# Softmax steps spread over three loop steps, and a gate load issued once, in a hybrid attention layer

## The chip, the cores and the metric

The kernel runs on one core of a Trainium2 chip. The metric is the device time of one execution in microseconds (us), lower is better. A core has five engines with their own instruction queues: TensorE (PE, matrix multiplications, with weight loads shown apart as PEld), VectorE (DVE), ScalarE (ACT), GpSimd (POOL) and SyncE (SP). In this kernel SP issues nearly all the DMA transfers. Each queue runs in order: an instruction that waits holds up everything behind it on its engine.

## The reference

One layer of a streaming encoder over 1024 prompt tokens and 64 new tokens of a running stream, all in float32. After a root-mean-square norm, one projection of 1024 to 6144 columns gives the queries, keys, values and a SiLU gate z for two attention branches of 8 heads of 64, and two gates per channel:

```python
h = rms_norm(x, norm_w) @ w_in
sb_q, sb_k, sb_v, sb_z, cb_q, cb_k, cb_v, cb_z, g_sb, g_cb = jnp.split(h, SPLIT_POINTS, axis=-1)
```

The first branch ("sb") is stick-breaking attention: each weight is a sigmoid times the product of (1 - sigmoid) over the keys between. The second ("cb") is softmax attention over a band of nine chunks of 64 keys with a clipped relative-position bias:

```python
s = jnp.where(mask, s + bias, NEG_INF)
p = jax.nn.softmax(s, axis=-1).astype(v.dtype)
return jnp.einsum("...hqk,...khd->...qhd", p, v)
```

The branches are merged and projected out:

```python
b_sb = (o_sb.reshape(lead + (WIDTH_SB,)) * jax.nn.silu(z_sb)) @ w_proj_sb
b_cb = (o_cb.reshape(lead + (WIDTH_CB,)) * jax.nn.silu(z_cb)) @ w_proj_cb
h = jax.nn.sigmoid(g_sb) * b_sb + jax.nn.sigmoid(g_cb) * b_cb
return x + h @ w_out
```

## The kernel before

Large matrices are split into a rounded high part and a remainder ("hi" and "lo"; `whi`, `wlo`, `xa`, `xm`, `xb`), and each product is three matrix multiplications: hi by hi, hi by lo, lo by hi. ScalarE makes the hi part of a weight tile (L115), GpSimd or VectorE subtracts to get the lo part (L122).

The kernel runs in this order: input projections (to about 398 us), then one long loop over attention tiles, then the second branch's projection (L926), then the output projection (L1429, L1465). What concerns us is the loop. Its list `seq` holds first all tiles of the first branch and then 68 tiles of the second: four pairs of heads, for each the 64 new tokens (t = 8) and eight blocks of 128 queries for each of two heads. In the code each loop step i does, in this order:

- `qk(i)`: the scores of tile i into PSUM (L1035). For the second branch VectorE takes them out of PSUM, adds bias and finds the running minimum (L1041, in two halves when the tile has over 512 keys; bias and queries carry a minus sign, so that the minimum stands for the softmax's maximum), and ScalarE makes the exponential in place with its sum (L1045). The tile is called `be`, the small statistics tile `sm`.
- `mid(i - 1)`: for the first branch the scan and the product (L1055, L1056), for the second the reciprocal of the sum (L1058) and the scaling of the tile (L1059).
- `fill`: a number of matrix multiplications of other work, taken one after another from a generator, so that TensorE has something to do while a tile is on its way through the other engines. The generator first runs the rest of the input projection (L782, results `sg`), and then `proj_sb`, the projection of the first branch's output (L882).
- `av`: when a block of queries is complete, weights times values (L1126) and the product with z (L1131), stored to DRAM (`d_ocb`).
- `tr(i - 3)`: TensorE transposes tile i - 3 (L1087), ScalarE and VectorE take turns copying it out of PSUM (L1096, L1098).
- the rest of the step's `fill`.

The `be` tiles have four buffers, the score tiles in PSUM (`z`) three, the transposed tiles (`pt`) two.

`proj_sb` goes through twelve pieces j, four pairs of column blocks by three stretches of tokens (384, 384 and 320). Each piece has two halves `uu`, each of twelve matrix multiplications into one of two PSUM accumulators (`acc`), which VectorE multiplies by the gate (L886) into a large tile `xm`. The gate tile `gt` of a piece, two blocks wide, comes back from DRAM (`d_gsb`, L862, by `load_gate`) in two DMAs. The tile has two buffers. `proj_sb` calls `load(j + 1)` twice: at the start of piece j, and again after the first half. Each call allots a tile and issues its two DMAs; the second call's tile is the one that piece j + 1 reads.

When the attention loop is done, what is left of `proj_sb` is filled in between loading the second branch's output (`ot`, L839) and splitting it into hi (L843, ScalarE) and lo (L848, by turns GpSimd and VectorE), for three stretches of tokens. The tile `ot` has two buffers there. These loads stand on the same SP queue as the gates', and the VectorE subtractions L848 stand on the same queue as the multiplications L886. In the built program the order on VectorE there is: L886 of piece 9 (first half), two L848, L886 of piece 9 (second half), L886 of piece 10 (first half), two L848, L886 of piece 10 (second half), two L886 of piece 11, two L848.

Of the kernel before, what the change touches and what calls it, by code (L numbers as in the profile page):

```python
# [10 lines left out]
AF = mybir.ActivationFunctionType  # L11
# [21 lines left out]
def hybrid_step_kernel(ctx: ExitStack, tc: tile.TileContext, x_prompt, x_sample, c_sbk, c_sbv, c_cbk, c_cbv,  # L33
# [3 lines left out]
    V, A, G, TE, SP = nc.vector, nc.scalar, nc.gpsimd, nc.tensor, nc.sync  # L37
# [15 lines left out]
    def rows(t):  # L53
        return 128 if t < 8 else NS
# [46 lines left out]
    class Weights:  # L101
# [5 lines left out]
        def load(self, key, pool, src, shape, extra="", nx=1):  # L107
            raw = pool.tile(shape, F32, name="wraw" + extra, bufs=nx if extra else 2)
            SP.dma_start(raw, src)
            self.raw[key] = (raw, pool, shape, extra)  # L110
# [87 lines left out]
    with ExitStack() as ph:  # L198
# [251 lines left out]
        for i in range(nb):  # L450
            for ti, t in enumerate(TO):
                r = rows(t)
# [91 lines left out]
    with ExitStack() as ph:  # L544
# [70 lines left out]
        for i in range(len(pairs)):  # L615
            bank, s1, u2, u3 = {}, {}, {}, {}
            for s in range(7):
                n = 7 * i + s
# [92 lines left out]
    SQ, KS, VP, BI, st, wT, zts = {}, {}, {}, {}, {}, {}, {}  # L711
# [98 lines left out]
    def og(b, s, p):  # L810
        return xhl[s][s][:, p] if b == "sb" else late["og"][s][:, p]

    def tb(u):
        return late["tbt"][:, u]
# [43 lines left out]
    def load_gate(pool, name, key, us, ci):  # L858
        a, e = CH[ci]
        gts[key] = pool.tile([128, 2, 384], F32, name=name, bufs=2)  # L860
        for w, d in enumerate(us):
            SP.dma_start(gts[key][:, w, :e - a], d[:, a:e])  # L862

    def proj_sb(pool):
        load = lambda j: j < 12 and load_gate(pool, "gt", j, d_g["sb"][2 * (j // 3):2 * (j // 3) + 2], j % 3)
        for j in range(12):
            i, ci = divmod(j, 3)
            wh, wl = W.sp["p", i]
            a, e = CH[ci]
            load(j + 1)  # L870
            if ci == 0:
                load_proj(i + 2)
            if ci == 1:
                W.split(("p", i + 1))
            gt = gts.pop(j)
            for uu in range(2):
                cw = slice(uu * 128, uu * 128 + 128)
                ps = psF.tile([128, 512], F32, name="acc")
                for p in range(NPAIR):
                    gh, gl = og("sb", 0, p), og("sb", 1, p)  # L880
                    for m, (w, g) in enumerate(((wh, gh), (wh, gl), (wl, gh))):
                        TE.matmul(ps[:, :e - a], w[:, p, cw], g[:, a:e], start=p == 0 and m == 0,  # L882
                                  stop=p == NPAIR - 1 and m == 2)
                        if p < NPAIR - 1 or m < 2:
                            yield 1
                V.tensor_tensor(out=tb(2 * i + uu)[:, a:e], in0=ps[:, :e - a], in1=gt[:, uu, :e - a], op=OP.mult)  # L886
                if uu == 0:
                    load(j + 1)
                yield 1

    def load_gcb(j):
# [95 lines left out]
    def fill(n):  # L987
        n += owed[0]
        owed[0] = 0
        while n > 0:  # L990
# [9 lines left out]
    seq = [(b, p, t, hd) for b in ("sb", "cb") for p in range(NPAIR) for t in [8] + list(range(8))  # L1000
           for hd in range(2) if t < 8 or hd == 0]

    def band(b, t):
        if t == 8:
            return 0, 576
        if b == "sb":
            return 0, (t + 1) * 128
        k0 = max(0, t - 4)
        return k0, (t + 1 - k0) * 128

    def qk(i):
        b, p, t, hd = seq[i]
        key = (b, p)
        r = 128
        k0, n = band(b, t)
        hs = [(0, n)] if n <= 512 else [(0, n // 2), (n // 2, n)]
        be = am.tile([128, NP], F32, name="be", bufs=4)
        if t == 8:
            s, ks, q0 = SQ[key, 3], KS[key, 1], 0
        else:  # L1020
            s, ks, q0 = SQ[key, t // 3], KS[key, 0], (t % 3) * 128
        if b == "sb":
            kp = ax.tile([128, NP + 2], F32, name="kp", bufs=3)
            G.memset(kp[:r, n:n + 1], 0.0)
        else:
            kp = am.tile([128, 4], F32, name="sm", bufs=6)
            bt = BI[2 * p + hd] if t < 8 else BI["s", p]
            off = 0 if t == 8 else 640 - n
        for j, (x, y) in enumerate(hs):
            z = psZ.tile([128, 512], F32, name="z")  # L1030
            o = k0 * 128
            m = y - x
            parts = [(2 * h + e, h) for h in ((0, 1) if t == 8 else (hd,)) for e in range(2)]
            for e, h in parts:
                TE.matmul(z[:, :m], s[:, e, q0:q0 + 128], ks[:, h, o + x:o + y], start=e == parts[0][0],  # L1035
                          stop=e == parts[-1][0])
            if b == "sb":
                A.activation(kp[:r, x:y], z[:r, :m], AF.Sigmoid, scale=-0.125)
                A.activation(be[:r, x:y], z[:r, :m], AF.Sigmoid, scale=0.125)
            else:  # L1040
                V.tensor_tensor_reduce(be[:r, x:y], z[:r, :m], bt[:r, off + x:off + y], 1.0,  # L1041
                                       BIG if j == 0 else kp[:r, j - 1:j], OP.add, OP.min, kp[:r, j:j + 1])
        if b == "cb":
            j = len(hs) - 1
            A.activation(be[:r, :n], be[:r, :n], AF.Exp, bias=kp[:r, j:j + 1], scale=-1.0, accum_out=kp[:r, 2:3])  # L1045
        st[i] = (be, kp)

    def mid(i):
        b, p, t, hd = seq[i]
        r = 128  # L1050
        k0, n = band(b, t)
        be, kp = st[i]
        if b == "sb":
            im = ims[:] if t == 8 else imp[:, NP - n:NP]
            V.tensor_tensor_scan(kp[:r, n - 1::-1], kp[:r, n - 1::-1], im[:, ::-1], 0.0, op0=OP.mult, op1=OP.add)  # L1055
            V.tensor_tensor(out=be[:r, :n], in0=be[:r, :n], in1=kp[:r, 1:n + 1], op=OP.mult)  # L1056
        else:
            V.reciprocal(kp[:r, 3:4], kp[:r, 2:3])  # L1058
            V.tensor_scalar(be[:r, :n], be[:r, :n], kp[:r, 3:4], None, op0=OP.mult)  # L1059
# [41 lines left out]
    def load_z(b, p, j):  # L1101
        zt = am.tile([128, 256], F32, name="zt", bufs=3)
        nq = 256 if j < 4 else 64
        SP.dma_start(zt[:, :nq], d_z[b][p][:, 256 * j:256 * j + nq])
        zts[b, p, j] = zt
# [53 lines left out]
    def load_bias(h):  # L1159
        bt = ab.tile([128, 640], F32, name="bias", bufs=4)  # L1160
        src = d_rb[h][0:1, 127:128]
        SP.dma_start(bt, bass.AP(tensor=src.tensor, offset=src.offset, ap=[[767, 128], [1, 640]]))
        G.memset(bt[0:64, 576:640], BIG)
        G.memset(bt[64:128, 0:64], BIG)
        BI[h] = bt
        if h % 2:
            bs = BI["s", h // 2] = ab.tile([128, 576], F32, name="bsm", bufs=1)
            for w in range(2):
                src = d_rb[h - 1 + w][0:1, 127:128]
                SP.dma_start(bs[64 * w:64 * w + 64], bass.AP(tensor=src.tensor, offset=src.offset,  # L1170
                                                             ap=[[767, 64], [1, 576]]))
# [16 lines left out]
    for i in range(len(seq) + LAG + 1):  # L1188
        m = 0
        if i < len(seq):  # L1190
            b, p, t, hd = seq[i]
            if b == "cb" and p == 0 and t == 8 and hd == 0:
                sbx.close()
                yst = ExitStack()
                late["y"] = yst.enter_context(tc.tile_pool(name="ay", bufs=2))
            if (b, p, t, hd) == ("sb", 3, 6, 0):
                load_bias(0)
                load_bias(1)
            qk(i)
            if hd == 0:  # L1200
                if t % 2 == 1 or t == 8 and (b, p) != ("sb", 0):
                    load_z(b, p, t // 2 if t < 8 else 4)
                prefetch(b, p, t)
            acc += amount[b] * wt[b](band(b, t)[1]) / tot[b]
            if (b, p, t) == ("cb", 0, 8):
                acc += 12
            m = int(acc) - emitted
            emitted += m
        if 0 < i <= len(seq):
            mid(i - 1)  # L1210
        flush()
        if i < len(seq) and seq[i][:3] == ("cb", 0, 1) and hd == 1:
            late["sb"] = True
        fill(m // 2)
        while avq:
            av(*avq.pop(0))
        if 0 <= i - LAG < len(seq):
            tr(i - LAG)
            b, p, t, hd = seq[i - LAG]
            if t == 8 or hd == 1 and t % 2 == 1:  # L1220
                avq.append((b, p, t // 2 if t < 8 else 4))
        fill(m - m // 2)
# [117 lines left out]
    hs = ow1.tile([128, KT, 128], F32R, name="hs", bufs=1)  # L1340
# [61 lines left out]
    for i in range(2):  # L1402
# [3 lines left out]
        for q, s in enumerate(OP_):  # L1406
            n = 8 * i + q
# [48 lines left out]
            for s_, wh, wl in ([] if n == 0 else [(0,) + first, (3, wh, wl)] if n == 1 else  # L1456
                               [(s, wh, wl)] if s in (0, 3, "b", 5) else []):
                w = 0 if s_ in (0, 3) else 1
                r = 0 if s_ in (0, "b") else 1
# [55 lines left out]
```

## Time and profile before

| | us |
|---|---|
| median of 3 runs | 998.18 (997.74 to 999.14) |
| the profiled execution | 996.75 |
| its span in the profile | 995.0 |
| TensorE busy | 971.9 |
| VectorE busy | 655.2 |
| ScalarE busy | 461.0 |
| GpSimd busy | 325.5 |

The lines L... in a profile are those of the kernel before. A group's row names the line, the engine, the operation, the tile written and the tiles read. A number in square brackets behind a row of the timeline is the time that the engine stood idle before it, and whose end released it. "PEclk" and "granted clock" give the share of its full clock that TensorE was granted. "SPq" is the queue of SyncE. A row of the view of waits gives the total, the number and the longest of a kind of wait. Start times in the timeline are counted from the start of the span.

### The profile page before, as it was taken

To read this page: it belongs to the slowest core of one execution; us is meant where nothing else is said; L and a number is where in the kernel's file an instruction comes from. 1 tells how busy PE (TensorE), PEld (TensorE's weight loads), DVE (VectorE), ACT (ScalarE), POOL (GpSimd) and SP (SyncE) were. 2 spreads that over 40 slices of the span, in tenths; PEclk is the share of its full clock that TensorE was granted. 3 is DMA by queue.
4 is the path that set the end of the run, shared out by engine and by line. 5 is a ranking of instruction groups with operands and counts; after the bars stand their busy time and mean duration, and the time that the engine had idled before them with its cause. 6 is when DMAs were issued, how large, how long until landed. Compare 5 with 4: busy or idle time off the path is not lost.

```text
span 995.0 us, 20010 instructions
## 1 busy us (share of the span) xinstructions
PE 971.9 (98%) x7472; PEld 928.7 (93%) x7472; DVE 655.2 (66%) x1200; ACT 461.0 (46%) x1038; POOL 325.5 (33%) x336
## 2 busy tenths in 40 slices
PE   5999999999999999999999999999999999899998
PEld 5999999999999999989988889899989898799998
DVE  5456674795455554189787988576657774589745
ACT  5534443444344433277676656444444433365320
POOL 3276663215445543211111101120103102286641
PEclk9999999999999999999999999999999999999999
DMA  6726577434656332697565657575667754852732
GB/s 228 234 93 222 190 245 254 153 97 138 200 151 197 113 95 83 176 237 199 142 172 158 165 155 193 136 200 149 188 183 236 226 162 149 265 172 93 214 125 84
DMA packets 181506, 171.02 MB, mean 172 GB/s; under 512 B 35040, under 2 KB 167264, under 8 KB 181280
## 3 DMA queue, kind: packets, MB, share of 16 engines
q1 hardware_dynamic: 172688, 161.41, 54.2%
q10 hardware_dynamic: 8720, 8.33, 2.6%
q8 instruction: 59, 0.97, 0.4%
q14 instruction: 39, 0.32, 0.1%
HBM read 110.96 MB, written 58.72 MB: 171 GB/s over the span
## 4 chain that ended last, share of the span: by engine, by line
PE 93%; DVE 2%; DMA 2%; ACT 1%; issue 1%; POOL 0%; SPq 0%; DVEq 0%; ACTq 0%
PE acc L464 19%; PE acc L782 18%; PE b L634 17%; PE b L1429 8%; PE o L1126 7%; PE z L1035 7%; PE pt L1087 6%; PE b L926 5%; PE acc L882 4%; DVE kp L1055 1%; PE pk L349 1%; DMA wrawx<-in_w_in_dram 1%; PE pt L277 1%; PE acc L1465 1%; PE acc L595 0%
## 5 line engine op out<-in xcount | busy, mean ns | idle before, releaser
L122 POOL TENSOR_TENSOR wlo<-wraw,whi 128x1024 fp32r<-128x1024 f32 x30 | 73.5, 2451 | 235.2 <-ACT whi L115 221.5
L782 PE MATMUL acc<-xm,whi 128*128 128x384 f32 (+1 forms) x384 | 129.1, 337 | 0.0
L1087 PE MATMUL pt<-ident,be 128*128 128x128 f32 (+1 forms) x568 | 87.6, 278 | 4.1 <-DVE wT L1098 3.0
L1055 DVE TENSOR_TENSOR_SCAN kp<-kp,imp 128x128 f32<-128x128 f32 (+7 forms) x64 | 90.0, 1407 | 0.1
L1045 ACT ACTIVATE be<-be,sm 128x640 f32<-128x640 f32 (+5 forms) x68 | 47.7, 702 | 89.3 <-DVE sm L1041 54.5
L1035 PE MATMUL z<-ks,sq 128*128 128x320 f32 (+5 forms) x384 | 83.3, 325 | 0.0
L1096 ACT ACTIVATE wT<-pt 128x512 f32<-128x512 f32 (+3 forms) x125 | 57.9, 477 | 54.0 <-PE pt L1087 53.4
L1087 PEld LDWEIGHTS pt<-ident,be 128*128 128x128 f32 (+1 forms) x568 | 66.4, 140 | 14.6 <-issue 5.3
L464 PE MATMUL acc<-whi,xa 128*128 128x256 f32 x256 | 74.2, 292 | 0.0
L782 PEld LDWEIGHTS acc<-xm,whi 128*128 128x128 f32 x384 | 72.4, 189 | 1.1
L464 PE MATMUL acc<-wlox,xm 128*128 128x256 f32 x256 | 70.7, 278 | 0.0
L464 PE MATMUL acc<-whi,xm 128*128 128x256 f32 x256 | 70.7, 278 | 0.0
L464 PE MATMUL acc<-wlo,xa 128*128 128x256 f32 x256 | 70.7, 278 | 0.0
L464 PE MATMUL acc<-whix,xb 128*128 128x256 f32 x256 | 70.6, 278 | 0.0
L464 PE MATMUL acc<-whix,xm 128*128 128x256 f32 x256 | 70.6, 278 | 0.0
L1035 PEld LDWEIGHTS z<-ks,sq 128*128 128x128 f32 x384 | 65.6, 188 | 1.1
L1056 DVE TENSOR_TENSOR be<-be,kp 128x128 f32<-128x128 f32 (+8 forms) x68 | 59.2, 871 | 9.1
L1126 PE MATMUL o<-wT,vp 128*64 128x256 f32 (+1 forms) x608 | 65.1, 356 | 0.0
L782 PE MATMUL acc<-xa,whi 128*128 128x384 f32 (+1 forms) x192 | 64.7, 337 | 0.0
L782 PE MATMUL acc<-xa,wlo 128*128 128x384 f32 (+1 forms) x192 | 64.6, 337 | 0.0
L782 PE MATMUL acc<-xb,whi 128*128 128x384 f32 (+1 forms) x192 | 64.4, 335 | 0.0
L782 PE MATMUL acc<-xm,wlo 128*128 128x384 f32 (+1 forms) x192 | 64.4, 335 | 0.0
(300 smaller groups left out, 2919.5 us busy)
## 6 DMA issues: line engine op xcount, KB each, us to landing
wraw<-in_w_in_dram SPq DMA_DIRECT2D x35, 512.0 KB, 4.7
wrawx<-in_w_in_dram SPq DMA_DIRECT2D x13, 512.0 KB, 4.4
sq<-d_qsbT SPq DMA_DIRECT2D x32, 192.0 KB, 4.2
sq<-d_qcbT SPq DMA_DIRECT2D x32, 192.0 KB, 3.6
gt<-d_gsb SPq DMA_DIRECT2D x30, 192.0 KB, 3.1
xt<-in_x_prompt_dram SPq DMA_DIRECT2D x8, 512.0 KB, 5.6
d_kcbT<-hl SPq DMA_DIRECT2D x8, 512.0 KB, 4.5
d_qcbT<-hl SPq DMA_DIRECT2D x8, 512.0 KB, 5.2
```

The costliest lines, as they stand in the source:

```text
L122: (eng or G).tensor_tensor(out=l, in0=raw, in1=h[:].bitcast(F32), op=OP.subtract)
L464: TE.matmul(ps, x, w, start=m == 0, stop=m == len(steps) - 1)
L634: TE.matmul(ps[:, :m], w[:, hl_, k], right[s](x)[:, k, a:b], start=s < 3 and k == 0 and e == 0, stop=k == 3 and e == 2, skip_group_check=s ...
L782: TE.matmul(ps[:, :b - a], w[:, k], xk(x, k)[:, a:b], start=k == 0 and n == 0, stop=k == KT - 1 and n == 2)
L926: TE.matmul(pp[uu][:, :n], w[:, p, uu * 128:uu * 128 + 128], g[:, a:e], start=p == 0 and m == 0, stop=p == NPAIR - 1 and m == 2)
L1035: TE.matmul(z[:, :m], s[:, e, q0:q0 + 128], ks[:, h, o + x:o + y], start=e == parts[0][0], stop=e == parts[-1][0])
L1055: V.tensor_tensor_scan(kp[:r, n - 1::-1], kp[:r, n - 1::-1], im[:, ::-1], 0.0, op0=OP.mult, op1=OP.add)
L1056: V.tensor_tensor(out=be[:r, :n], in0=be[:r, :n], in1=kp[:r, 1:n + 1], op=OP.mult)
L1087: TE.transpose(pt[:kr, x, :r], be[:r, kb * 128:kb * 128 + kr], ident[:r, :r])
L1096: A.activation(w[:, sl:sl + m, q0:q0 + r], pt[:, :m, :r], AF.Copy)
L1126: TE.matmul(o[hd * 64:hd * 64 + 64, c0:c1], vv[:kr, kb, hd * 64:hd * 64 + 64], wT[b, p, j, hd, s // 4][:kr, s % 4, c0:c1] if j < 4 else wT ...
L1429: TE.matmul(ps[:, t], left[s](xs_, k)[:, ts_], wt_[:, k], start=s < 3 and t == k == e == 0, stop=k == 3 and e == 2, skip_group_check=s > 2 ...
```

## The change

In the second branch, the exponential leaves `qk` and becomes a function of its own, `soft`, which the loop calls for tile i - 1 before `qk(i)`. The second branch's `mid` is called for tile i - 2, also before `qk(i)`. For the first branch `mid(i - 1)` keeps its place behind `qk(i)`. The transposes stay at `tr(i - 3)`. So on ScalarE's queue the exponential of a tile stands one step later than before, ahead of the next tile's work; on VectorE's queue the reciprocal and the scaling of a tile stand one step later, and ahead of the bias and minimum of tile i, not behind them.

In `proj_sb`, the second `load(j + 1)` is taken out: 22 of the 46 DMAs that read `d_gsb`. The order of the instructions on TensorE and on GpSimd is the same as before.

```diff
                 V.tensor_tensor(out=tb(2 * i + uu)[:, a:e], in0=ps[:, :e - a], in1=gt[:, uu, :e - a], op=OP.mult)
-                if uu == 0:
-                    load(j + 1)
                 yield 1
...
-        if b == "cb":
-            j = len(hs) - 1
-            A.activation(be[:r, :n], be[:r, :n], AF.Exp, bias=kp[:r, j:j + 1], scale=-1.0, accum_out=kp[:r, 2:3])
         st[i] = (be, kp)
+
+    def soft(i):
+        n = band(*seq[i][::2])[1]
+        be, kp = st[i]
+        j = 1 if n > 512 else 0
+        A.activation(be[:, :n], be[:, :n], AF.Exp, bias=kp[:, j:j + 1], scale=-1.0, accum_out=kp[:, 2:3])
...
+        if 0 < i <= len(seq) and seq[i - 1][0] == "cb":
+            soft(i - 1)
+        if 1 < i <= len(seq) + 1 and seq[i - 2][0] == "cb":
+            mid(i - 2)
+        if i < len(seq):
             qk(i)
...
-        if 0 < i <= len(seq):
+        if 0 < i <= len(seq) and seq[i - 1][0] == "sb":
             mid(i - 1)
         flush()
```

## The prediction

> **What bounds the kernel now.** I read the page first: its shares by engine, then the chain that ended last.
>
> ```profile
> span 995.0 us, 20010 instructions
> PE 971.9 (98%) x7472; PEld 928.7 (93%) x7472; DVE 655.2 (66%) x1200; ACT 461.0 (46%) x1038; POOL 325.5 (33%) x336
> PE 93%; DVE 2%; DMA 2%; ACT 1%; issue 1%; POOL 0%; SPq 0%; DVEq 0%; ACTq 0%
> ```
>
> TensorE is busy for 971.9 of 995.0 us. A change that leaves its matmuls as they are can only win from the 23.1 us in which it stands still, or from matmuls that run at a lower clock. So I next asked for the busy time by stage (second branch's attention, last part of the first branch's projection, second projection, output projection) and for whom TensorE waits.
>
> ```profile
> 613.00:836.00 223.00, 220.44 (x1604) 200.82 (x1604) 150.55 (x440) 101.12 (x241) 32.36 (x28) 1.00 0.63 181
> 836.00:860.00 24.00, 19.45 (x115) 17.88 (x112) 8.63 (x14) 5.02 (x9) 6.42 (x5) 0.96 0.69 213
> 860.00:910.00 50.00, 50.00 (x308) 50.00 (x308) 43.01 (x57) 29.88 (x51) 33.55 (x27) 0.98 0.54 170
> 910.00:995.00 85.00, 81.06 (x716) 80.86 (x714) 50.33 (x62) 22.21 (x30) 37.33 (x16) 1.00 0.44 140
> ...
> PE acc L882 <- DVE xm L886: 4.5, 4, 3.2
> PE pt L1087 <- DVE wT L1098: 1.7, 3, 1.1
> PE pt L1087 <- ACT wT L1096: 0.9, 2, 0.5
> ```
>
> Columns of the first rows: stretch, length, then busy time of PE, PEld, DVE, ACT and POOL, granted clock, DMA share, GB/s. The change touches the first two stretches. In them TensorE idles 223.00 - 220.44 = 2.56 us and 24.00 - 19.45 = 4.55 us. The last rows say on whom: 4.5 us in four waits of the first branch's projection (L882) for the gate multiplication (L886), 1.7 + 0.9 us in the attention for copies out of PSUM. Nothing else on TensorE is to be had: 7.1 us, and what the clock loses.
>
> **Part one: each gate loaded once.** The multiplication L886 needs its gate tile, and the two accumulators of L882 come free only after it. The four waits, the DMA queue beside them, and the chain through this place:
>
> ```profile
> L862 SPq DMA_DIRECT2D gt<-d_gsb x46: 319/422/998, 752.4 to 855.9; - x46
> 845.89 0.45 PE L882 MATMUL acc<-xa,whi 128*128 128x384 f32 x1 [0.51 <-DVE xm L886]
> 848.55 0.44 PE L882 MATMUL acc<-xa,whi 128*128 128x384 f32 x1 [0.30 <-DVE xm L886]
> 851.50 0.41 PE L882 MATMUL acc<-xa,whi 128*128 128x320 f32 x1 [0.57 <-DVE xm L886]
> 856.68 0.41 PE L882 MATMUL acc<-xa,whi 128*128 128x320 f32 x1 [3.16 <-DVE xm L886]
> 840.53 0.43 SPq L862 DMA_DIRECT2D gt<-d_gsb  x1
> 841.74 3.45 DMA gt<-d_gsb
> 844.28 1.36 SPq L862 DMA_DIRECT2D gt<-d_gsb  x2
> 848.52 0.81 SPq L862 DMA_DIRECT2D gt<-d_gsb  x2
> 849.43 1.80 SPq L839 DMA_DIRECT2D ot<-d_ocb  x4
> 849.85 3.75 DMA ot<-d_ocb
> 853.62 1.57 ACT L843 ACTIVATE og<-ot 128x384 fp32r<-128x384 f32 x3 [0.84 <-DMA ot<-d_ocb]
> 845.75 2.27 DVE L848 TENSOR_TENSOR og<-ot,og 128x384 fp32r<-128x384 f32 x2
> 844.76 2.38 POOL L122 TENSOR_TENSOR wlo<-wraw,whi 128x1024 fp32r<-128x1024 f32 x1 [0.94 <-ACT whi L115]
> ```
>
> The 46 issues are 2 for the first gate tile and 2 x 2 for each of the 11 others; 22 of them go. Read in time: the first copy of gate 9 is issued until 840.96, its second copy at 841.74, and this second copy, in flight for 3.45 us, holds the multiplication until 845.28. The first copy of gate 10 is issued at 844.28, so gate 9's first copy had landed by about then. The second copy of gate 10 is issued at 848.52, and only behind it the four tiles of the second branch's output (849.43, ot). The last of these, 3.75 us in flight by the chain, lands at 853.60. Then ScalarE rounds, VectorE subtracts (L848), and in VectorE's order the next L886 stands behind that subtraction: it starts at 856.09, 2.49 us after the landing, and TensorE has stood still for 3.16 us.
>
> With one copy: gate 9 is there by 844.28, its multiplication 1.0 us earlier, and the 0.51 wait goes. Gate 10's only copy takes the place at 841.74 and lands, at the same 3.45 us, by 845.2. The first half of gate 10's matmuls ran from 845.89 to 848.25 (848.55 less the wait of 0.30); without the 0.51 they end at about 847.7, so that copy is hidden. The ot tiles wait only for their buffers, that is for the two subtractions L848 now at 845.75 to 848.02. These start 1.0 earlier too, but the second shares its time with POOL's L122 (844.76 to 847.14), which doesn't move, so its end lies between 847.0 and 848.0. The second pair of ot, whose last issue was at 850.80 (849.43 + 1.80 less one issue of 0.43), now has it at 847.5 to 848.5; with 2.8 us (853.60 - 850.80) to 3.75 us in flight it lands at 850.3 to 852.2, between 1.4 and 3.3 us earlier. Add the same 2.49 us: TensorE resumes 1.4 to 3.3 us before 856.68. I take 2.8, nearer the upper end, since the trace's own last transfer took 2.8. TensorE's wait there shrinks to about 1.3 us, because the 0.57 wait before it goes as well and its work ends earlier. The wait of 0.30 stays. The second copies of gates 1 to 8 lie in the attention, where no wait of TensorE is put down to L886; taking them out wins nothing there.
>
> A second effect lies behind it:
>
> ```profile
> 784.00:786.00 2.00, 1.10 (x8) 1.10 (x9) 1.97 (x8) 0.45 (x3) 0.06 (x1) 1.00 0.95 267
> 858.00:859.00 1.00, 1.00 (x6) 1.00 (x6) 0.28 (x1) 0.00 (x0) 0.00 (x0) 0.61 0.98 306
> 859.00:860.00 1.00, 1.00 (x4) 1.00 (x4) 0.49 (x1) 0.00 (x0) 0.00 (x0) 0.50 0.89 266
> 860.00:861.00 1.00, 1.00 (x4) 1.00 (x4) 0.00 (x0) 0.88 (x1) 0.00 (x0) 0.50 0.87 283
> 861.00:862.00 1.00, 1.00 (x5) 1.00 (x5) 0.00 (x0) 0.99 (x2) 0.00 (x0) 0.68 0.91 280
> ```
>
> About 1.4 us after the long wait the granted clock falls to half for some 3.4 us: 0.39 + 0.50 + 0.50 + 0.32 = 1.71 us of TensorE's work lost. A wait of 1.06 us (784 to 785) left it at 1.00. The wait I forecast, 1.3 us, is far nearer 1.06 than 3.16, so I take the 1.7 us as won, with 0 as the other end. [...]
>
> Downstream the lead must survive. From 860 to 910 TensorE never waits (50.00 of 50.00), but VectorE is nearly full there (43.01). The tightest place:
>
> ```profile
> 922.21 2.40 POOL L1292 TENSOR_TENSOR wo<-wo,wo 128x1024 fp32r<-128x1024 f32 x1 [4.37 <-ACT wo L1291]
> 920.34 16.32 PE b L1429 x144
> ```
>
> POOL's weights are done at 924.61. In this run of 144 matmuls (16.32 / 144 = 0.113 us each) TensorE needs them in the 51st, at 926.0: 1.4 us of slack. The chain of gates and ot behind POOL's work comes 2.8 earlier, TensorE 2.8 + 1.7 = 4.5; the difference of 1.7 overruns the slack by 0.3. I charge 0.2 (0 to 0.3).
>
> **Part two: the exponential one step later, the normalising two.** No instruction is added; none on SP or POOL moves, and TensorE's order is unchanged.
>
> ```profile
> ACT be L1045 <- DVE sm L1041: 54.5, 45, 2.5
> DVE be L1041 <- PE z L1035: 40.8, 50, 2.0
> L1045 ACT ACTIVATE be<-be,sm x68: 401/777/837, 616.3 to 827.6; 128x640 f32<-128x640 f32 x32, 128x128 f32<-128x128 f32 x8, 128x256 f32<-128x256 f32 x8, 128x384 f32<-128x384 f32 x8
> L1059 DVE TENSOR_SCALAR be<-be,sm x68: 285/553/2501, 621.2 to 831.2; 128x640 f32<-128x640 f32 x32, 128x128 f32<-128x128 f32 x8, 128x256 f32<-128x256 f32 x8, 128x384 f32<-128x384 f32 x8
> L115 ACT ACTIVATE whi<-wraw 128x1024 fp32r<-128x1024 f32 x10 | 10.5, 1049 | 0.0
> 782.13 2.25 DVE L1059 TENSOR_SCALAR be<-be,sm 128x576 f32<-128x576 f32 x1
> 781.69 2.38 POOL L122 TENSOR_TENSOR wlo<-wraw,whi 128x1024 fp32r<-128x1024 f32 x1 [2.68 <-ACT whi L115]
> 784.90 0.44 PE L1087 MATMUL pt<-ident,be 128*128 128x128 f32 x2 [1.06 <-DVE wT L1098]
> 623.46 1.14 PE L1087 MATMUL pt<-ident,be 128*128 128x128 f32 x8 [0.52 <-ACT wT L1096]
> ```
>
> Now ScalarE stands at each exponential until VectorE has the minimum of the same step (54.5 us), with its PSUM copies (L1096) queued behind; VectorE waits 40.8 us for the scores. Afterwards the exponential finds its minimum a step old, and the scaling runs while VectorE would wait for scores. A step lasts 223 / 68 = 3.3 us, the exponential at most 0.84, the scaling 0.55 in the median: the transposes, still three steps behind, find their tile scaled a step ahead. The move costs nothing while that slack covers it; without it, at the end of the branch where no projection fills the steps, one exponential and one scaling (1.4 us) could show once. What is won is bounded by the 2.56 us. 0.52 hangs on ScalarE's queue and should go. 1.06 hangs on a scaling stretched to 2.25 us beside POOL's subtraction: the order behind it changes (next the score evacuation, then the copy), so it can go or come back at another step (the L115 row counts 10 weight tiles rounded in this stage, each followed by such a pass of POOL). The rest are the emptied steps at the end. I take 0.5 (ends: 2.6 won, 2 lost by two more such collisions of 1.06).
>
> **Sum.** 2.8 + 1.7 + 0.5 - 0.2 = 4.8 us. The profiled execution took 996.75 us (span 995.0), so 992.0. The timed runs have their median at 998.18, 1.43 above it: 993.4.
>
> **Rivals.**
> 1. The clock falls all the same. Short waits remain close together, 0.30 and 1.3. [...] For it: the dip came 1.4 us after the resumption, so it is not tied to one wait alone. Against: many small waits in the attention at clock 1.00. Then the 1.7 isn't won and the 0.2 isn't charged: 998.18 - 3.3 = 994.9. Chance 0.14.
> 2. The gates are early but something else holds the multiplication: the ot tiles, or POOL's L122 beside L848. For it: the 3.16 wait ends on ot, not on a gate. Then only 0.51 + 0.57 go, the clock still dips, and the attention gives 0 to 0.5: about 997.0. Chance 0.13.
> 3. Slower: in the attention POOL's L122 (10 passes) meets the scaling in every pass, as in 782.13, and what stands behind it is now the evacuation of the scores and the copies. If each pass costs 1.06 us on TensorE, that is 10.6 less the 1.6 already paid: 9.0 lost against 4.3 won elsewhere, 998.18 + 4.7 = 1002.9. It decides from six such passes on (6 x 1.06 is more than 4.3 + 1.6). Against: scalings of up to 2.50 us are there now, and all of TensorE's waits for copies are 2.6 us. Chance 0.07.
> 4. All waits of both stretches go: 7.1 + 1.7 = 8.8, 989.4. Chance 0.10. That the change doesn't do what it says is excluded for the gates by the 46 issues.
>
> **How the numbers follow.** My forecast has 0.56; its own range, from the ends of its terms (2.8: 1.4 to 3.3; 0.5: -1 to 1.5; 1.7), is 991.5 to 996.3. The whole range must leave out no more than 2 in 10: up to 997.0 for rival 2, down to 990.5 for half of rival 4. A measurement of this kernel tells 0.2%, 2 us, from no change. Faster, below 996.2: forecast, rivals 1 and 4, and a little of 2: 0.81. Same: most of rival 2: 0.11. Slower: rival 3 and accidents: 0.08.
>
> **What would show it.** 24 gate issues in place of 46; TensorE's waits for L886 at 2 us or less in place of 4.5 and the longest under 2; granted clock 1.00 after the last of them; ScalarE's wait of 54.5 near nothing; TensorE's waits in the attention at 2.6 or less. The forecast is wrong if the ot tiles land no earlier, if the clock dips, or if waits for PSUM copies grow past 4 us.

## The result and the profile after

The changed kernel takes 990.14 us (median of 4 runs, 989.93 to 992.98). Beside it on the same chip the kernel before took 998.4 (997.74 to 999.14). The ratio is 0.9924 with a 95% interval of 0.9904 to 0.9943: 8.3 us faster, where 4.8 were forecast. The unaltered kernel run again later on another chip gave 991.31 (988.84 to 994.83), ratio 0.9931 (0.9913 to 0.9948). The profiled execution took 989.93, with a span of 988.1 where the one before had 995.0. That profile of the kernel before is one of its faster executions (996.75, against medians of 998.2 to 998.7), so the spans differ by less (6.9) than the medians.

The page of the kernel after: span, busy times, and the shares of the chain that ended last.

```profile
span 988.1 us, 20002 instructions
PE 968.8 (98%) x7472; PEld 927.1 (94%) x7472; DVE 649.3 (66%) x1200; ACT 458.4 (46%) x1038; POOL 325.1 (33%) x336
PE 93%; DMA 3%; DVE 2%; SPq 1%; issue 0%; POOL 0%; ACT 0%; DVEq 0%; ACTq 0%
```

TensorE carries the same work (x7472) and still bounds the kernel. The stages (columns as before the change):

```profile
613.00:836.00 223.00, 222.15 (x1622) 203.12 (x1621) 144.46 (x441) 99.24 (x241) 32.45 (x28) 1.00 0.59 168
836.00:860.00 24.00, 21.30 (x129) 21.04 (x128) 9.60 (x16) 9.06 (x16) 9.04 (x7) 1.00 0.73 220
860.00:910.00 50.00, 50.00 (x333) 50.00 (x332) 46.68 (x58) 30.01 (x53) 36.68 (x28) 1.00 0.55 172
```

TensorE's idle time is 0.85 us in the attention (2.56 before) and 2.70 in the tail (4.55). The granted clock stays at 1.00 in these stages. Who waits for whom, the first row over the span and the others in the window 613 to 836:

```profile
PE acc L882 <- DVE xm L886: 2.7, 1, 2.7
...
PE pt L1088 <- DVE wT L1099: 0.4, 1, 0.4
PE pt L1088 <- ACT wT L1097: 0.4, 1, 0.4
ACT be L1047 <- DVE sm L1039: 8.8, 10, 1.9
DVE be L1039 <- PE z L1033: 22.2, 36, 2.0
ACT wT L1097 <- PE pt L1088: 87.5, 44, 4.8
```

Four waits for the gate multiplication have become one, and the waits for copies out of PSUM have fallen from 1.7 + 0.9 us to 0.4 + 0.4. ScalarE's 54.5 us at the exponential (now L1047) are 8.8, and VectorE's 40.8 us for scores are 22.2. ScalarE's idle time hasn't gone, it has moved: it now waits 87.5 us for the transposes (25.2 before), where it holds up nobody.

To place the gain I cut the span at three landmarks on TensorE: the second branch's first scores, the start of its last weights-times-values, and the first matmul of the second projection. The timeline of the kernel before, then of the kernel after:

```profile
614.44 1.21 PE L1035 MATMUL z<-kss,sqs 128*128 128x288 f32 x8
834.48 2.81 PE L1126 MATMUL o<-wT,vp 128*64 128x256 f32 x24
858.79 0.84 PE L926 MATMUL b<-og,whi 128*128 128x384 f32 x2
```

```profile
614.25 1.21 PE L1033 MATMUL z<-kss,sqs 128*128 128x288 f32 x8
832.05 2.81 PE L1127 MATMUL o<-wT,vp 128*64 128x256 f32 x24
853.45 0.51 PE L924 MATMUL b<-og,whi 128*128 128x384 f32 x2
```

The stretch between the first two landmarks is called the attention below, the next the tail, and what follows the rest. The attention went from 220.04 (834.48 - 614.44) to 217.80, the tail from 24.31 to 21.40, the rest, to the end of the span, from 136.21 to 134.65. The gain of 6.9 in the span is 0.2 before the first landmark + 2.2 + 2.9 + 1.6. The same stretches of every kernel below, each from its one profiled execution:

| kernel | median | ratio (95%) | attention | tail | rest |
|---|---|---|---|---|---|
| before | 998.4 | | 220.04 | 24.31 | 136.21 |
| after | 990.14 | 0.9924 (0.9904, 0.9943) | 217.80 | 21.40 | 134.65 |
| after_again | 991.31 | 0.9931 (0.9913, 0.9948) | 218.86 | 20.77 | 135.50 |
| gate_only | 992.60 | 0.9946 (0.9934, 0.9958) | 220.04 | 20.63 | 135.04 |
| gate_late | 993.03 | 0.9945 (0.9929, 0.9961) | 220.48 | 20.52 | 135.66 |
| soft_only | 996.79 | 0.9984 (0.9975, 0.9992) | 217.59 | 26.90 | 135.64 |
| before_keepwarm | 996.61 | 0.9980 (0.9971, 0.9989) | 220.03 | 24.47 | 134.81 |
| exp_only | 992.23 | 0.9939 (0.9922, 0.9956) | 220.08 | 20.61 | 135.05 |
| scale_behind | 993.45 | 0.9953 (0.9938, 0.9969) | 220.77 | 20.56 | 134.67 |
| scale_first | 997.02 | 0.9986 (0.9975, 0.9996) | 224.07 | 20.30 | 134.65 |
| before_split_v | 998.98 (one run) | | 220.09 | 25.54 | 136.86 |
| og_later | 989.47 | 0.9910 (0.9897, 0.9923) | 217.71 | 18.44 | 135.53 |
| og_later_again | 988.41 | 0.9899 (0.9885, 0.9913) | 217.83 | 18.45 | 134.96 |

The ratios are against runs of the kernel before on the same chip, whose medians were 998.4 to 998.7. The two profiles of the changed kernel differ by 1.1 in the attention and 0.6 in the tail: differences below that say nothing by themselves. Over all profiles the attention is 217.6 to 218.9 in the five that have both moves of the softmax, and 220.0 to 220.5 in the five that have neither. Line numbers in the experiments are shifted by a few against the kernel before or after.

### The profile page after: what moved, and what is told of

It is laid out like the page before. It is cut to its first block, busy times and chain, and to the rows that moved or that the text cites. A ratio compares the mean times of both kernels' runs of the same rounds, so it can differ in the third digit from the quotient of the medians.

```text
span 988.1 us, 20002 instructions
## 1 busy us (share of the span) xinstructions
PE 968.8 (98%) x7472; PEld 927.1 (94%) x7472; DVE 649.3 (66%) x1200; ACT 458.4 (46%) x1038; POOL 325.1 (33%) x336
## 4 chain that ended last, share of the span: by engine, by line
PE 93%; DMA 3%; DVE 2%; SPq 1%; issue 0%; POOL 0%; ACT 0%; DVEq 0%; ACTq 0%
PE acc L464 19%; PE acc L782 18%; PE b L634 17%; PE b L1435 8%; PE o L1127 7%; PE z L1033 6%; PE pt L1088 6%; PE b L924 5%; PE acc L882 3%; DMA gt<-d_gsb 1%; DVE kp L1056 1%; PE pk L349 1%; DMA wrawx<-in_w_in_dram 1%; PE pt L277 1%; PE acc L1471 1%; DMA ot<-d_osb 1%
## 5 line engine op out<-in xcount | busy, mean ns | idle before, releaser
L1036 ACT ACTIVATE kp<-z 128x384 f32<-128x384 f32 (+6 forms) x104 | 51.2, 493 | 27.3 <-PE z L1033 26.2
```

## The experiments

**The two parts apart.** The gate part alone, and the softmax part alone:

```diff
# gate_only, against before
-                if uu == 0:
-                    load(j + 1)
# soft_only, against after
+                if uu == 0:
+                    load(j + 1)
```

> The change's first part alone: the second load of each gate is taken out, the softmax steps stay where they were. Theory (the two parts add up): all of the tail's gain is here. TensorE resumes 2.8 us earlier in the last piece of the first branch's projection, its longest wait for the gate multiplication is about 2.7 us in place of 3.16, the granted clock stays at 1.00 behind it, worth another 1.7 us; the attention keeps its waits of 0.52 and 1.06. Span 995.0 - 4.5 = 990.5, median 993.7. Rival (the tail is gained only because the shorter attention shifts the queues against each other): the long wait stays near 3.2, the clock dips, and the span is 993 or more.

> The change's second part alone: exponential one step and normalising two steps later, each gate still loaded twice. Theory: the waits of 0.52 and 1.06 in the attention go, the last product with the values starts 2.4 us earlier than before, the tail stays as before with its 3.16 us wait and the clock dip. Span 995.0 - 2.4 = 992.6, median 995.8. Rival (the gate loads' traffic and queue made the attention's gain): the waits stay, span 994 to 995.

The gates alone give 6.0 us (998.58 beside it, to 992.60), the softmax part alone 1.8. The sum, 7.8, is near the 8.3 measured for both. The gates' gain lies where it was forecast: tail 24.31 to 20.63, rest 136.21 to 135.04, attention unchanged. The wait that is left there is 1.93 us, shorter than the 2.7 I expected. In the softmax part alone the attention wins 2.45, but with the second copies still there its profiled execution gives it all back in the tail. The timeline, the waits, two transfers from the chain and two windows of soft_only there (the windows between, all near 0.50, left out):

```profile
856.09 0.63 PE L882 MATMUL acc<-xa,whi 128*128 128x320 f32 x1 [4.04 <-DVE xm L886]
```

```profile
PE acc L882 <- DVE xm L886: 6.2, 3, 4.0
```

```profile
840.18 4.97 DMA gt<-d_gsb
...
848.03 5.02 DMA ot<-d_ocb
```

```profile
854.00:855.00 1.00, 0.00 (x0) 0.00 (x0) 0.60 (x2) 0.55 (x2) 0.84 (x1) 0.56 0.04 13
...
860.00:861.00 1.00, 1.00 (x4) 1.00 (x4) 0.19 (x1) 0.99 (x2) 0.00 (x0) 0.53 0.65 218
```

TensorE came to the tail 1.9 sooner (832.56 for 834.48), but the loads hardly did: issued earlier, they were 5 us in flight and landed at 845.15 and 853.05, where before it was 845.19 and 853.60. So the waits for L886 grew from 4.5 to 6.2, and half the clock was gone from 854 to 861. The two spans are equal (995.0 and 995.1), yet the median falls by 1.8: the profile of the kernel before is a fast execution of it (996.75, median 998.58 beside this run), that of soft_only an average one (996.87, median 996.79). So how often the tail takes the gain back isn't shown.

**Which of the two copies.** The first call taken out and the second kept:

```diff
# gate_late, against before
-            load(j + 1)
```

> The kernel before with one load of each gate, but the other one: the call at the start of a piece is out, the call after the first half stays. Theory (what costs is the second copy, which holds the queue until the first has landed or the buffer comes free, with the other loads behind it): as good as taking out the second call, median 992 to 993.5, granted clock 1.00 behind the longest wait. Rival (what counts is that the load that is read comes half a piece earlier): the gates come late as before, waits for the gate multiplication of 4 us or more, median 996 to 998.

The tail takes 20.52, as in gate_only (20.63), and the ratios are equal within their intervals. It isn't the earlier place that wins; a second copy ahead of `ot` in the queue is what cost. SyncE's own waits from 765 to 862 us, in the kernel before and then after, show how:

```profile
SPq L862 <- DMA gt<-d_gsb: 18.4, 12, 2.9
```

```profile
SPq L862 <- DMA gt<-d_gsb: 0.2, 1, 0.2
```

Twelve times SyncE stood with a gate load until another gate load had landed, 18.4 us in all, with everything behind it held. It isn't the lighter traffic: in the window 835 to 860 the median time from issue to landing of the 192 KB loads has risen, from 3.3 to 4.3 us for `ot` and from 3.5 to 4.9 for the gates.

**The clock.** The kernel before with 14 unread matmuls put into the long wait; nothing reads their PSUM tile, and the multiplication that TensorE waits for stays where it is:

```diff
# before_keepwarm, against before
+NDUM = 14
...
+                if j == 11 and uu == 1:
+                    dm = late["dum"].tile([128, 512], F32, name="dum")
+                    for m in range(NDUM):
+                        TE.matmul(dm[:, :e - a], wh[:, 0, cw], og("sb", 0, 0)[:, a:e], start=m == 0, stop=m == NDUM - 1)
...
```

> The kernel before, with 14 matmuls more ahead of the last half piece of the first branch's projection, into a PSUM tile that nobody reads. They take 14 x 0.147 = 2.1 us and fit into the 3.16 us in which TensorE stands still there, so that it resumes at the same time but has idled only about 1.1 us. Theory (the half clock follows from the length of that wait): the granted clock stays at 1.00 and the second projection starts at full rate, 1.7 us won: span 993.3, median 996.5. Rival (the dip has another cause): the clock falls to half as before and the span is 995.0 or more.

A window of before_keepwarm:

```profile
858.00:860.00 2.00, 2.00 (x14) 2.00 (x15) 0.51 (x2) 0.00 (x0) 0.00 (x0) 1.00 0.89 264
```

TensorE's wait there is 1.20 us in place of 3.16. The clock stays at 1.00, the tail is as long as before (24.47), and the rest is shorter by 1.40. So the idle stretch caused the dip, and the dip cost about 1.4 in this profile (2.0 by the medians), where I had worked out 1.71. In two of its ten timed runs the mean clock is 0.998 all the same.

**What carries the attention's gain.** Two theories. A: ScalarE's queue; its PSUM copies stood behind an exponential that waited for the minimum. B: VectorE's order; it must not have a late scaling between the scores and what TensorE waits for. exp_only takes just the exponential a step later; scale_behind takes both later as the change does, but puts the scaling behind the minima; scale_first leaves the exponential in its step and puts only the scaling ahead of the next minima.

```diff
# exp_only, against after
-        if 1 < i <= len(seq) + 1 and seq[i - 2][0] == "cb":
-            mid(i - 2)
...
-        if 0 < i <= len(seq) and seq[i - 1][0] == "sb":
+        if 0 < i <= len(seq):
             mid(i - 1)
# scale_behind, against after
-        if 1 < i <= len(seq) + 1 and seq[i - 2][0] == "cb":
-            mid(i - 2)
         if i < len(seq):
             qk(i)
...
+        if 1 < i <= len(seq) + 1 and seq[i - 2][0] == "cb":
+            mid(i - 2)
# scale_first, against after
         if 0 < i <= len(seq) and seq[i - 1][0] == "cb":
-            soft(i - 1)
-        if 1 < i <= len(seq) + 1 and seq[i - 2][0] == "cb":
-            mid(i - 2)
+            mid(i - 1)
         if i < len(seq):
             qk(i)
+            if seq[i][0] == "cb":
+                soft(i)
```

> The changed kernel, but reciprocal and scaling go back to their old place: one step after the scores, behind the bias and minimum of the next tile; only the exponential is a step later. Measure: the time from the first scores of the second branch to its last product with the values, 220.0 us with the old order (before, and with the gates alone changed), 217.6 to 217.8 with the new one. Theory A (what counts is that ScalarE's copies no longer stand behind an exponential that waits for VectorE): 217.8 here too, span as the changed kernel's. Theory B (what counts is VectorE's order, the stretched scalings no longer ahead of the copies): 219 to 219.5, the wait of 1.06 near 785 us comes back, and the median is 1.2 to 1.7 above the changed kernel's.

> The changed kernel, but the reciprocal and scaling, still two steps after the scores, stand behind the bias and minimum of the newest tile on VectorE, not ahead of them. Theory A (ScalarE's queue): 217.8 from first scores to last product. Theory B (place on VectorE, since a scaling stretched beside GpSimd's subtraction then stands right ahead of the copies out of PSUM again): 218.5 to 219.5, with a wait of about 1 us near 785.

> The changed kernel with the exponential put back into its own step, behind the minimum; only the reciprocal and the scaling stay ahead of the next tile's minima on VectorE (one step later than before, not two). If the place of the scaling on VectorE alone makes the gain in the attention: the stretch from the branch's first scores to its last weights-times-values takes 217.5 to 218.3 us as in the changed kernel (217.80), and the time is within 1 us of it (989.5 to 991). If it needs both, the scaling ahead and a step between exponential and scaling: VectorE now waits at the head of each step for the exponential of the step before, and the stretch takes 219.5 to 220.5 us, the time 992 to 993.

None of the three has the attention's gain: 220.08, 220.77 and 224.07 against 217.80, each from one profile and each longer than my theories allowed (219.5, 219.5 and 220.5 at most). Theory A as I held it falls with exp_only: ScalarE was freed, the wait of 0.52 at 623 went, and the stretch is as long as before. Its medians are also no better than the gate part alone (992.23 and 992.60). In scale_behind the transposes wait for the scaling itself; its waits and timeline:

```profile
PE pt L1088 <- DVE be L1060: 1.2, 2, 0.8
```

```profile
780.22 2.74 DVE L1060 TENSOR_SCALAR be<-be,sm 128x640 f32<-128x640 f32 x1
```

But theory B alone falls too, with scale_first, which moves the scaling ahead and loses 4 us. Its waits in the window 613 to 838, and a row of its VectorE timeline:

```profile
ACT be L1047 <- DVE sm L1039: 96.0, 65, 3.0
...
DVE sm L1059 <- ACT be L1047: 12.6, 18, 1.1
```

```profile
785.50 2.48 DVE L1060 TENSOR_SCALAR be<-be,sm 128x576 f32<-128x576 f32 x1
```

Here VectorE stands at the head of a step for the exponential (12.6 us), the next minima come later for it, and ScalarE waits 96.0 us for these. TensorE's waits for the copies of the transposed tiles come to 4.8 us in this window (2.6 before), the longest, 1.6, ends at 788.71, shortly behind the scaling at 785.50, which is stretched to 2.48. What wins is the pair: the scaling ahead of the minima, and the exponential a step before it, so that nobody stands for it. I can't name every part of what exp_only loses: up to 799 us it is ahead of the kernel before by 1.0 and loses that again by the end, and in that last part the profile lists, beyond a wait of 0.36 that both kernels have, only waits of 0.20 and 0.58 (0.39 before).

**The stretched scaling.** The wait of 1.06 at 784.90 hung on a scaling beside a pass of POOL. The next kernel is the one before with that one pass moved from POOL to VectorE:

```diff
# before_split_v, against before
-                W.split(("p", i + 1))
+                W.split(("p", i + 1), V if i == 0 else None)
```

> The kernel before, with one of the weight subtractions moved from GpSimd to VectorE: the one that runs from 781.69 to 784.07 beside the scaling of 2.25 us. Theory (GpSimd's pass stretches the scaling, and that makes TensorE's wait of 1.06 at 784.90): no scaling over 1 us there, the wait gone or below 0.3 although VectorE has 1.2 us more to do, first scores to last product 219.0. Rival (the scaling was stretched by something else, or the emptied short steps alone make the wait): the wait stays near 1, 220.0 or more.

The timeline of before_split_v at that place:

```profile
781.91 1.22 DVE L122 TENSOR_TENSOR wlo<-wraw,whi 128x1024 fp32r<-128x1024 f32 x1 [0.46 <-ACT whi L115]
...
784.05 0.52 DVE L1059 TENSOR_SCALAR be<-be,sm 128x576 f32<-128x576 f32 x1
...
783.79 0.44 PE L1087 MATMUL pt<-ident,be 128*128 128x128 f32 x2 [1.15 <-DVE wT L1098]
```

The scaling takes 0.52 us in place of 2.25, so POOL's pass did stretch it. But the wait stays (1.15), because the subtraction now takes 1.22 us of VectorE right ahead of the copy that TensorE waits for (783.05 to 783.73). The run shows the cause of the stretch; whether the wait would go with neither in the way it can't tell. In the kernel after the stretch is still there, without a wait at its place (timeline, VectorE then POOL):

```profile
779.50 2.17 DVE L1060 TENSOR_SCALAR be<-be,sm 128x640 f32<-128x640 f32 x1
...
778.93 2.39 POOL L122 TENSOR_TENSOR wlo<-wraw,whi 128x1024 fp32r<-128x1024 f32 x1 [1.65 <-ACT whi L115]
```

In after_again a wait for a copy came back there, 0.91 us long, and that profile's attention is 1.1 longer.

**The wait that is left.** In the kernel after, the rest of `proj_sb` taken out wholly ahead of the second pair of `ot` splits, so that L886 no longer stands behind L848; and the same once more beside the unaltered change:

```diff
# og_later, against after
-        fill((46, 24, 100000)[ci])
+        fill((46, 100000, 0)[ci])
```

> The changed kernel, with the rest of the first branch's projection put ahead of the splitting of the second stretch of the second branch's output, so that VectorE's gate multiplications no longer stand behind the subtractions that wait for that load. Theory: the wait of 2.70 us that the changed kernel still has goes, or shrinks to what the last gate's load takes: span 988.1 - 2 to 2.7 = 985.4 to 986, median about 988. Rival: the second projection then waits for the split that comes later, at its second piece, and the span stays at 988.

> The changed kernel unaltered, for a comparison on one chip. Both theories: 989.5 to 991.5 us.

> The changed kernel with the rest of the first branch's projection taken out wholly ahead of the second pair of output tiles' splits, as in og_later. If the 0.7 us between the medians of og_later and the changed kernel is more than scatter: 988.5 to 990, 0.5 to 1.2 below the changed kernel beside it. If the wait taken away comes back in full behind it: the same to 0.3 us.

The stage rows of og_later_again:

```profile
836.00:860.00 24.00, 24.00 (x147) 24.00 (x147) 9.63 (x19) 9.80 (x17) 8.62 (x7) 1.00 0.71 218
860.00:910.00 50.00, 50.00 (x339) 50.00 (x338) 45.81 (x59) 30.20 (x54) 37.89 (x28) 1.00 0.55 172
```

TensorE doesn't wait in the tail at all. Side by side the medians are 988.41 and 991.31; in the first comparison, which was not side by side, 989.47 and 990.14. The intervals of the two pairs still meet (0.9913 on the last chip), so the gain of some 1 to 3 us is likely, not certain. One thing speaks for it besides: the mean granted clock is 1.000 in all eight timed runs of it, and 0.998 in four of the ten of the changed kernel. It is the fastest version here.

## Why the prediction was right, and where its sizes were off

The direction, the cause and the place were right; the size was not. I forecast 993.4 and measured 990.14, just below my low end of 990.5 (the repeat, 991.31, lies inside). Of the 3.3 us missing, 1.7 are the attention's term. Another 1.2 come from the step from profile to median: I added 1.43, as before, but the profiled execution after lies only 0.2 below its median. What that step is made of no run here shows. The other terms make up the remaining 0.4.

**Gate term, 2.8.** Measured 2.9 in the tail of the pair of profiles, 3.7 in gate_only. The mechanism held: the gates are issued once, and `ot` no longer stands behind a second copy. The issues (grouped by line), then the tail's timeline, of the kernel after:

```profile
L862 SPq DMA_DIRECT2D gt<-d_gsb x24: 319/423/1731, 751.9 to 845.6; - x24
```

```profile
851.59 0.41 PE L882 MATMUL acc<-xa,whi 128*128 128x320 f32 x1 [2.70 <-DVE xm L886]
848.84 2.23 DVE L848 TENSOR_TENSOR og<-ot,og 128x384 fp32r<-128x384 f32 x2 [3.19 <-ACT og L843]
850.99 0.94 DVE L886 TENSOR_TENSOR xm<-acc,gt 128x384 f32<-128x384 f32 x2
847.77 2.04 ACT L843 ACTIVATE og<-ot 128x384 fp32r<-128x384 f32 x4 [5.13 <-DMA ot<-d_ocb]
842.83 2.08 SPq L839 DMA_DIRECT2D ot<-d_ocb  x4
845.06 0.82 SPq L862 DMA_DIRECT2D gt<-d_gsb  x2
```

TensorE resumes 5.09 us earlier (851.59 for 856.68), 2.43 of it because the attention ended earlier; that leaves 2.66, close to 2.8. The steps inside were off, and cancelled. The issue of `ot` in gate_only, whose attention is as long as before:

```profile
845.57 1.76 SPq L839 DMA_DIRECT2D ot<-d_ocb  x4
```

I had the last `ot` issue at 847.5 to 848.5; it was at 846.90 (845.57 + 1.76 less one issue of 0.43). But I took 2.8 us in flight, which I had read wrongly: the landing at 853.60 belongs to the load issued at 849.85, 3.75 us earlier, not to the last issue at 850.80. In the kernel after the first of them lands 4.9 us after its issue (847.77 - 842.83). Behind it ScalarE's four roundings now stand back to back (2.04): only the first has a wait ahead of it. The multiplication still stands behind L848, as forecast.

**"The wait shrinks to about 1.3 us, and the 0.30 stays."** Wrong. The 0.30 went with the 0.51 and the 0.57, TensorE came to the last half piece 2.20 earlier in the tail instead of 1.1, and so it stood 2.70 there (3.16 - 2.66 + 2.20). Of these 2.20, 1.38 are the three waits as listed. The other 0.8 is what a break costs beyond its listed wait. TensorE's timeline before, around the first of the three:

```profile
845.04 0.34 PE L882 MATMUL acc<-xa,wlo 128*128 128x384 f32 x1
845.89 0.45 PE L882 MATMUL acc<-xa,whi 128*128 128x384 f32 x1 [0.51 <-DVE xm L886]
846.17 0.34 PE L882 MATMUL acc<-xb,whi 128*128 128x384 f32 x1
```

In an unbroken stream matmuls of 384 columns start some 0.17 us apart, each before the one ahead has ended. Here two starts are 0.85 apart and the next follows after 0.28: 0.78 lost for a listed wait of 0.51. The same sum over all three breaks gives 2.2. So a wait costs some 0.27 us more here than its row shows, and I had counted waits at their rows. TensorE's total for L886, 2.7, and its longest wait, 2.7, missed my bounds of 2.

**Clock, 1.7, and the charge of 0.2.** The net forecast for the rest was 1.5, measured 1.6. The reason that I gave for it failed, though: I counted on a wait of 1.3 us, and it was 2.70, far nearer to 3.16. Why the clock stayed at 1.00 behind it in this profile no run shows. Nor is rival 1 out for every execution. The mean granted clock was 0.998 in four of the ten timed runs of the changed kernel (991.30, 992.98, 993.21 and 994.83 us), as in the profile before with its dip, and 0.999 or 1.000 in the other six (988.84 to 991.31). None of the four was profiled, so where their clock fell isn't known; in the profile after, the fall at the end of the span makes up only 0.0006 (half of 1.1 us, in 988.1). The charge of 0.2 can't be told apart from the rest.

**Attention, 0.5 (ends -2 and 2.6).** This is the mis-sized term: 2.2 in the profile, 1.2 in the repeat, 1.8 by soft_only's median. In the sum for the range I had used -1 to 1.5 for it, narrower than the ends I had argued for, and the 2.2 lies outside these. (By its own terms the low end there is 991.7 rather than 991.5.) I took a fifth of the possible gain because I expected the wait of 1.06 to come back elsewhere and the emptied last steps to stay. The first came back only in the repeat. In the last steps the waits of 0.38 and 0.36 did stay. I had also given the 0.52 to ScalarE's queue, and exp_only bears that out: it goes there. The rest I left to chance, and it hangs on VectorE's order together with the added step, as the three kernels show.

**The other rivals.** Rival 2 (the `ot` tiles hold the multiplication anyway) describes what is left rather than what happened: they do hold it, but earlier by more than I feared. Rival 3 (POOL's passes) would have shown waits for copies beyond 4 us; they were 0.8 in the attention. In scale_first a scaling stretched to 2.48 us stands just ahead of the longest of these waits, 1.6 us; that a pass of POOL lay beside it there was not shown. Rival 4 (all waits go, 989.4) is nearest in time, but not in its reason: 2.7 us in the tail and 0.85 in the attention remain.

## What to carry to other kernels

Look for transfers whose data nobody reads: in an in-order DMA queue their cost isn't their own time but the start of whatever stands behind them, here 6 of 8 us. When a softmax is spread over loop steps, move the whole chain: an exponential moved without its scaling won nothing here, and a scaling moved ahead without a step of slack lost 4 us of attention. After a wait has gone, look at what stands ahead of the waiting instruction on its own engine; here reordering the two took the last wait of the tail away. And don't trust a clock that stayed up in one profile: compare it over the timed runs.

## What was unexpected of the hardware

The fall of the granted clock came at no fixed time from the wait. In the kernel before, the rows at 858 and 861 (0.61 and 0.68) put the half clock from 858.22 to 861.64. In soft_only the rows above (0.56 and 0.53) put it from 854.12 to 860.94. It began about 4.7 us after TensorE stopped in the first and 2.1 after in the second, where TensorE hadn't yet resumed. The longest wait of TensorE in the tail and the clock behind its beginning, each from one profile:

| kernel | longest wait, us | it ends at | granted clock |
|---|---|---|---|
| soft_only | 4.04 | 856.09 | 0.50 from 854.12 to 860.94 |
| before_split_v | 3.32 | 857.53 | 0.55 in 858 to 860, 0.59 in 860 to 862 |
| before | 3.16 | 856.68 | 0.50 from 858.22 to 861.64 |
| after | 2.70 | 851.59 | 1.00 |
| gate_only | 1.93 | 853.70 | 1.00 |
| exp_only | 1.90 | 853.78 | 1.00 |
| before_keepwarm | 1.50 | 847.71 | 1.00 |

Windows of before_split_v, then of the kernel after, with the clock in the last column but two:

```profile
856.00:858.00 2.00, 0.47 (x3) 0.47 (x4) 1.48 (x2) 0.00 (x0) 0.60 (x1) 1.00 0.38 111
858.00:860.00 2.00, 2.00 (x10) 2.00 (x9) 0.49 (x1) 0.00 (x0) 0.00 (x0) 0.55 0.81 254
860.00:862.00 2.00, 2.00 (x10) 2.00 (x8) 0.49 (x1) 1.40 (x2) 0.00 (x0) 0.59 0.82 239
```

```profile
850.00:852.00 2.00, 0.41 (x3) 0.42 (x4) 1.93 (x3) 0.00 (x0) 0.65 (x1) 1.00 0.00 0
852.00:854.00 2.00, 2.00 (x15) 2.00 (x15) 0.35 (x1) 0.00 (x0) 0.00 (x0) 1.00 0.68 211
854.00:856.00 2.00, 2.00 (x13) 2.00 (x12) 0.14 (x1) 1.49 (x2) 0.00 (x0) 1.00 0.89 238
```

In these seven profiles the clock fell in the three with the longest waits. The length of a wait alone doesn't tell, though: at the start of the kernel before, TensorE stands 7.50 us until VectorE's first tile (L277 for L266), and the clock is 1.00 all the same in the first 10 us. What decides it was not shown. The clock falls once more at the end of both profiles, when TensorE is done: in the kernel before at 994.76 (0.88 in the window 994 to 995), in the kernel after at 987.0 (0.50 from there on).

Transfers of the same kind varied widely in flight: the `ot` load that the chain before showed took 3.75 us, and the first one after, 4.9. Removing loads did not make the remaining ones land sooner after their issue: the medians in the window 835 to 860 went from 3.3 to 4.3 us for `ot` and from 3.5 to 4.9 for the gates.
